# A hybrid attention and gating trunk on one core: forget gates, log-sum stores, output tiles' steps and the last row re-timed

## The chip, the core and the metric

The kernel runs on one core of a Trainium2 chip. The core has a matrix engine (PE, whose weight loads are listed as PEld), a vector engine (DVE), an activation engine (ACT), a general engine (POOL) and a sequencer (SP) that only issues transfers (DMAs). Each engine takes its instructions strictly in the order in which they stand in its queue, and waits where an operand or a buffer is not ready. The metric is the time of one execution in microseconds (us).

## The reference

One layer: an RMS norm and one input projection, then two token mixers side by side, one output projection of both with a residual, a SwiGLU feed-forward network with a residual, and a last RMS norm. There are 2048 tokens, 1024 features, 8 attention heads of 64, 8 gating groups of 64 and a hidden width of 2816. Everything is float32.

```python
xn = rms_norm(x, mix_norm_g[l])
q, k, v, f_logit, z = jnp.split(xn @ w_in[l], ...)
log_f = jax.nn.log_sigmoid(f_logit + b_f[l])
attn = forgetting_attention(q, k, v, log_f)      # softmax(q.k/8 + c[t] - c[s], s <= t) @ v, c = cumsum(log_f)
sgu = spatial_gating(gelu(z), sgu_ln_g[l], sgu_ln_b[l], w_s[l], b_s[l])
merged = concat([rms_norm(attn, out_norm_g[l, :512]), rms_norm(sgu, out_norm_g[l, 512:])])
x = x + merged @ w_out[l]
gate, up = jnp.split(rms_norm(x, ffn_norm_g[l]) @ w_gate_up[l], 2, axis=-1)
x = x + (silu(gate) * up) @ w_down[l]
return rms_norm(x, final_norm_g)
```

## The kernel before

A float32 operand is split into a high part (`hi_of`, a cast) and a low part (`lo_of`, the difference, line 131). A product takes three matmuls: high by high, high by low, low by high. The ACT mostly makes the high parts, the DVE the low ones. Python loops write the whole program out; a planner then sets the order of the instructions on each engine from its own model of their durations. `behind(i)` keeps what is written inside it behind instruction `i` on the same engine. Many helpers are Python generators: whoever calls `next` on one lets it write its instructions up to its next `yield`. So the number of `yield`s sets how many steps of the surrounding loop lie between two parts of a helper.

**Stage 1, the projection** (0 to about 315 us) takes four chunks `c` of 512 tokens. A chunk first makes its 8 rows of forget logits (lines 540 to 554) and stores them to `FD[c]` from ACT's queue. Then follow four tiles of q, four of k and, from the second chunk on, four of v, each 24 matmuls. After each tile `between` (line 430) moves two helpers by one step: `gates_`, which is `forget_rows(c)`, and `xg`, which prepares the next chunk's x (`Chunk.steps`, line 293). `forget_rows` loads the rows back as a tile `F` (line 315, issued by POOL) and computes the logarithm of the sigmoid on ACT and DVE (lines 320 to 328), later a cumulative sum on PE. In the meantime PE also takes, between the tiles' matmuls, the maxima of the chunk before (`one_max`, line 357): a matmul into one of two buffers `mx_ps`, and a DVE reduction (lines 362 and 365) that frees it.

**Stage 2** (to about 960 us) is 320 steps `n` (line 1242). A step is one key block of one head and query chunk: scores (`qk`, lines 735 and 736), an exponential and its two parts (738 to 742), a mask by POOL on the diagonal (748), and the products with v of the step before (`pv_of`, lines 768 to 773). Beside them run the gating branch (`gates`, with `z_proj`, `v_side` and `u_side`), and towards the end the output projection. When a head's query chunk is done, `fin` (line 777) copies the lower half of the sum (`lv`, whose first row is the log-sum's denominator), stores that row to `SD` from ACT's queue, and stores the numerator `nd` to `AT` from SP's. When all 8 heads of a query chunk `j` are done, it loads `SD[j]`, inverts it and stores it to `RD[j]`. `u_side` stores the transposed gating rows to `ST` from ACT's queue (line 1002).

From step `OPEN` = 260 on, two generators `out_prep(t, ...)`, for output tiles t = 0 and 1, move by one step each time (line 1295). Each loads `ST`, `AT` and, twice, `RD` (lines 1084 to 1089), multiplies (1092), squares on ACT (1094), adds on POOL (1097, 1098), sums over the partitions by a PE matmul (1111), takes the inverse root, and spreads it by a PE transpose (1116). For t = 0 and 1 the argument `space` is not None. `out_tiles` (line 1178) runs the output projection in groups of tiles; each of its group's 16 half steps moves the `out_prep` of the next tiles (t = 2 and 3 beside the first group) by one step.

**Stage 3, the feed-forward network** (to the end) uses 7 products in place of 8 for a 2 x 2 block product, n = 0 to 6 (line 1692). `Rows.evac(n)` adds a product into the rows `x`. The last group has a single item, for the rows t = 14 and 15. A finished row block goes to `Down.done`: the sum of its squares (ACT), an inverse root (DVE and POOL), a multiplication by it and by the norm's weights `finb` (DVE), and a store. t = 15 has its last addition at n = 5, t = 14 at n = 6; t = 14 is already treated in halves.

Of the kernel before, what the change touches and what calls it, by code (L numbers as in the profile page):

```python
# [8 lines left out]
F32 = mybir.dt.float32  # L9
F32R = mybir.dt.float32r  # L10
AF = mybir.ActivationFunctionType
ALU = mybir.AluOpType
# [4 lines left out]
P = 128  # L17
S = 2048
D = 1024
# [6 lines left out]
CH = 512  # L26
# [38 lines left out]
LEND = 276  # L65
LEAD = 14
ZF = 3
OPEN = 260
BURST = 6
ORATE = 2  # L70
FT = 9
# [4 lines left out]
NB = S // P  # L76
EPS = 1e-6
# [8 lines left out]
def trunk(ctx: ExitStack, tc: tile.TileContext, x, x_t, mix_g, w_in, b_f, ln_g, ln_b, w_st, b_st, on_g, w_out,  # L86
          ffn_g, w_gu, w_down, fin_g, c_mat, c_row, out):
    nc = tc.nc
# [4 lines left out]
    def T(pool, shape, dt, tag, **kw):  # L93
        n_t[0] += 1
        for tags, other in apart.get(id(pool), ()):
            if tag in tags:
                pool = other
        return pool.tile(shape, dt, tag=tag, name=f"{tag}_{n_t[0]}", **kw)
# [11 lines left out]
    def behind(*ins):  # L110

        s = ExitStack()
        for i in ins:
            s.enter_context(tc.issue_after(i.ins))
        return s
# [6 lines left out]
    ld = nc.sync.dma_start  # L122
# [36 lines left out]
    ST = [T(dram, [P, 4, P], F32, f"ST{t}") for t in range(NB)]  # L159
    AT = [T(dram, [P, 4, CH], F32, f"AT{c}") for c in range(NCH)]  # L160
    GD = [T(dram, [P, 4, CH], F32, f"GD{q}") for q in range(NCH)]
    SD = [T(dram, [H, CH], F32, f"SD{c}") for c in range(NCH)]
# [150 lines left out]
    def forget_rows(j):  # L313

        nc.gpsimd.dma_start(F[32 * j : 32 * j + 32, :], FD[j].rearrange("h (b t) -> b h t", t=P))
        for _ in range(1 if j else 2):
            yield
        sm = T(p1, [P, 8, P], F32, "v")
        ax, ex, u1, ln, er, ru, lf = (sm[:, i, :] for i in range(7))
        nc.scalar.activation(ax, F, AF.Abs)  # L320
        nc.scalar.activation(ex, ax, AF.Exp, scale=-1.0)
        nc.vector.tensor_scalar_add(u1, ex, 1.0)
        nc.scalar.activation(ln, u1, AF.Ln)
        nc.vector.scalar_tensor_tensor(er, u1, -1.0, ex, ALU.add, ALU.subtract)
        nc.vector.reciprocal(ru, u1)
        nc.vector.tensor_tensor(er, er, ru, ALU.mult)
        nc.vector.tensor_tensor(ln, ln, er, ALU.subtract)
        nc.vector.scalar_tensor_tensor(lf, F, 0.0, ln, ALU.min, ALU.subtract)
        for _ in range((3, 2, 1, 1)[j]):
            yield  # L330
        pl = T(ps1, [P, 4, P], F32, "tp")
        nc.tensor.transpose(pl[:, 0, :], lf, ident)
        sm2 = T(p1, [P, 4, P], F32, "fT", bufs=1)
        lfT, loc, nck = sm2[:, 0, :], sm2[:, 1, :], sm2[:, 2, :]
        nc.vector.tensor_copy(lfT, pl[:, 0, :])
        yield
        pl = T(ps1, [P, 4, P], F32, "tp")
        nc.tensor.matmul(pl[:, 1, :], lfT, tri, start=True, stop=True)
        nc.vector.tensor_copy(loc, pl[:, 1, :])
        yield  # L340
        pl = T(ps1, [P, 4, P], F32, "tp")
        nc.tensor.matmul(pl[:, 2, 0:1], cm[:, 1 + j, :], loc[:, P - 1 : P], start=True, stop=True)
        car = T(p1, [P, 1], F32, "car")
        nc.vector.tensor_copy(car, pl[:, 2, 0:1])
        nc.vector.tensor_scalar(nck, loc, car, -1.0, ALU.add, ALU.mult)
        augs = T(p1, [P, 2, P], F32R, "qh")
        nc.vector.tensor_copy(augs[:, 0, :], nck)
        lo_of(nc.vector, augs[:, 1, :], nck, augs[:, 0, :])
        n = 8 * (4 * j + 4)
        ldr(AUG[0:n, 2 * j : 2 * j + 2, :], augs[0:n])  # L350
# [185 lines left out]
    for c in range(NCH):  # L536
# [4 lines left out]
        n = 0  # L541
# [24 lines left out]
        for which, w in ((0, wq), (1, wk)):  # L566
            for pr in range(4):
                pm = T(ps1m, [P, CH], F32, "mm", bufs=4)
                n = 0
# [44 lines left out]
        for tt in range(4 if c else 0):  # L614
# [4 lines left out]
            a, b, _ = v_close(pm, xc, tt)  # L619
# [157 lines left out]
    def fin(h, j):  # L777
        pr, o = h // 2, (h % 2) * DH
        pv, _ = live.pop((h, j))
        nd, lv = T(p2, [DH, CH], F32, "nd", bufs=1), T(p2, [DH, CH], F32, "lv", bufs=1)  # L780
        nc.scalar.copy(lv, pv[DH:P])
        nc.scalar.dma_start(SD[j][h : h + 1], lv[0:1])
        nc.vector.scalar_tensor_tensor(nd, lv, m0[0:DH], pv[0:DH], ALU.mult, ALU.add)
        ld(AT[j][o : o + DH, pr, :], nd)
        heads[j] += 1
        if heads[j] == H:
            yield
            sr = T(p2, [P, H * CH // P], F32, "sr")
            ld(sr, SD[j].rearrange("h (a t) -> (h a) t", t=H * CH // P))
            yield  # L790
            yield
            yield
            nc.vector.reciprocal(sr, sr)
            ld(RD[j].rearrange("h (a t) -> (h a) t", t=H * CH // P), sr)
        yield
# [181 lines left out]
    def u_side(q, zr):  # L977

        yield
        yield  # L980
        ss = T(p2, [P, 4], F32, "ss2", bufs=1)
        m = mixes.pop(q)
        for cc in range(4):
            with behind(*newest):
                nc.vector.tensor_tensor(zr[:, cc, :], zr[:, cc, :], m[:, cc, :], ALU.mult)
                jk = T(p2, [P, CH], F32, "jk", bufs=1)
                nc.scalar.activation(jk, zr[:, cc, :], AF.Square, accum_out=ss[:, cc : cc + 1])
            yield
        rs = rsqrt(p2, ss, 1.0 / 512, "rs", n=4)
        yield  # L990
        last = q == NCH - 1
        if last:
            z4 = T(p2z, [P, 4, 4, P], F32, "zvh", bufs=1)
        for cc in range(4):
            nc.vector.tensor_scalar_mul(zr[:, cc, :], zr[:, cc, :], rs[:, cc : cc + 1])
            tp = T(ps2, [P, 4, P], F32, "mx_ps", bufs=NMX) if last else T(psz, [P, 4, P], F32, "z", bufs=NZ)
            for k in range(4):
                nc.tensor.transpose(tp[:, k, :], zr[:, cc, k * P : (k + 1) * P], ident)
            yield
            sT = z4[:, cc] if last else T(p2z, [P, 4, P], F32, ("wsth", "wstl")[cc % 2], bufs=1)  # L1000
            nc.scalar.copy(sT, tp)
            nc.scalar.dma_start(ST[4 * q + cc], sT)


    units = [(h, j) for h in range(H) for j in range(NCH)]
# [69 lines left out]
    first, o = [], [{} for _ in range(NB)]  # L1075

    def out_prep(t, o, space=None):
        c, sl = t // 4, slice((t % 4) * P, (t % 4 + 1) * P)
        r = raw4()
        if space is None:  # L1080
            rd = sq = T(pev, [P, 4, P], F32, "rd", bufs=3)
        else:
            rd, sq = space
        ld(r[:, 4:8, :], ST[t])
        ld(r[:, 0:4, :], AT[c][:, :, sl])

        for hh in range(2):
            ld(rd[hh * DH : (hh + 1) * DH],
               RD[c].rearrange("(pr o hh) t -> hh o pr t", hh=2, o=1)[hh, :, :, sl].broadcast_to([DH, 4, P]))
        for _ in range(4):  # L1090
            yield
        nc.vector.tensor_tensor(r[:, 0:4, :], r[:, 0:4, :], rd, ALU.mult)
        yield
# [11 lines left out]
            else:  # L1105
                ld(o["x"], x[t * P : (t + 1) * P, :])

        for _ in range(3 if space is None else 5):
            yield
        ps = E["tp"]()  # L1110
        nc.tensor.matmul(ps[:, 0, 0:1], sq[:, 0, :], ones_c, start=True, stop=True)
# [426 lines left out]
    class Down(Rows):  # L1538
# [18 lines left out]
        def evac(self, n):  # L1557
            super().evac(n)
            if (self.kb, self.tp, n) == (2, NB // 2 - 1, 3):

                xt = self.x[0][:, 0:CH]
                self.a = T(pev, [P, 1], F32, "a5")
                self.squares(xt, self.a)
                nc.vector.tensor_scalar(self.a, self.a, 1.0 / D, EPS, ALU.mult, ALU.add)
                nc.vector.tensor_tensor(xt, xt, finb[:, 0:CH], ALU.mult)

        def squares(self, xt, ss):
            jk = T(pev, [P, D], mybir.dt.bfloat16, "jk", bufs=1)
# [2 lines left out]
        def done(self, t, xt, at):  # L1571
            if self.kb < 2:
                ld(XA[t], xt)
                return
            ss = T(pev, [P, 1], F32, "ss4")
            o = out[t * P : (t + 1) * P, :]
            if t == NB - 2:
                right = xt[:, CH:]
                self.squares(right, ss)
                nc.vector.scalar_tensor_tensor(ss, ss, 1.0 / D, self.a, ALU.mult, ALU.add)  # L1580
                r = T(pev, [P, 1], F32, "r4r")
                nc.gpsimd.tensor_tensor(r, ss, mhalf[:, 0:1], ALU.pow)
                nc.vector.scalar_tensor_tensor(right, right, r, finb[:, CH:], ALU.mult, ALU.mult)
                ld(o[:, CH:], right)
                nc.scalar.activation(xt[:, 0:CH], xt[:, 0:CH], AF.Copy, scale=r)
                ld(o[:, 0:CH], xt[:, 0:CH])
                return
            while now[0] == at and at < len(grp) - 1:
                yield
            with behind(*copies if at < len(grp) - 1 else ()):  # L1590
                self.squares(xt, ss)
            yield
            r = rsqrt(pev, ss, 1.0 / D, "r4")
            if at == len(grp) - 1:
                yield
            nc.vector.scalar_tensor_tensor(xt, xt, r, finb, ALU.mult, ALU.mult)
            ld(o, xt)
            yield
# [93 lines left out]
    for q in range(len(slots)):  # L1692
# [35 lines left out]
            now[0] = p  # L1728
        tail = p == len(grp) - 1
        with behind(*[its[0].last] if tail and n else ()):  # L1730
            for _ in range((2, 2, 2, 2, 0, 1, 1)[n] if tail else len(its)):
                while posts and next(posts[0], 0) == 0:
                    posts.pop(0)
            if tail and n == 6:
                next(posts.pop(), None)
        if last:
            nextR[n] = next(fill)
        if sums and p:
# [50 lines left out]
```

## Time and profile before

| what | value |
|---|---|
| median of 3 runs | 2362.72 us (2359.24 to 2364.0) |
| the profiled execution's own time | 2363.86 us |
| its span, from first to last instruction | 2362.0 us |
| DVE busy | 1673.4 us (71%) |
| ACT busy | 1058.8 us (45%) |
| POOL busy | 609.8 us (26%) |
| bytes moved by DMA | 423.88 MB, mean 179 GB/s |
| mean granted PE clock | 0.998 of full |

The profile is of one execution. A row of the timeline gives the start and the duration in us, engine, line, operation, written and read tiles, shapes, and in brackets how long the engine was idle before and what ended that. "SPq" and "ACTq" are issues of transfers by those queues. A row of the waits gives the waiting instruction, what ended its waits, their sum in us, their number and the longest. A row of the windows gives the busy time of each engine in a stretch, with the number of instructions in brackets. A matmul is listed with about 0.39 us, but one starts about every 0.225 us.

### The profile page before, as it was taken

Reading aid. Unit: us, or ns where it says so; the run is one execution under the profiler, and the core shown is the slowest. Engines: PE = TensorE matmul, PEld = TensorE weight load, DVE = VectorE, ACT = ScalarE, POOL = GpSimd, SP = SyncE. Lnnn points to the kernel's source line nnn. Section 1 sums busy time; section 2 is a strip of 40 time slices with the busy share of each in tenths; the row PEclk is TensorE's granted clock in tenths of the full one; section 3 lists DMA queues with packets and bytes.
Section 4 is the critical chain, followed back from the end, with each engine's and each line's share of the span. In section 5 each row is a group of like instructions: output and inputs, shape, how many; then the busy total and the mean of one; then the engine's idle time right before and its main releaser. Section 6 shows DMA issues by size and latency. Waiting matters only on the chain.

```text
span 2362.0 us, 31692 instructions
## 1 busy us (share of the span) xinstructions
PE 2332.7 (99%) x10582; PEld 1893.4 (80%) x10582; DVE 1673.4 (71%) x2781; ACT 1058.8 (45%) x1771; POOL 609.8 (26%) x704
## 2 busy tenths in 40 slices
PE   9999999999999999999999999999999999999998
PEld 7787777777777777888888888888888888888886
DVE  6658668888888666566666666866666586685788
ACT  5322138777778766444323232532333252332433
POOL 1100012122211222221323223232323234353431
PEclk9999999999999999999999999999999999999999
DMA  8745667656677775674344544725454355574554
GB/s 271 282 153 200 203 198 210 186 152 170 178 201 241 222 227 171 212 222 153 108 142 148 164 143 125 230 82 148 120 152 134 98 187 192 189 257 169 190 195 149
DMA packets 375803, 423.88 MB, mean 179 GB/s; under 512 B 23941, under 2 KB 277573, under 8 KB 371673
## 3 DMA queue, kind: packets, MB, share of 16 engines
q1 hardware_dynamic: 359656, 378.62, 52.3%
q0 software_dynamic: 7616, 27.33, 3.3%
q10 hardware_dynamic: 8368, 15.91, 1.8%
q8 instruction: 85, 1.39, 0.2%
q14 instruction: 78, 0.63, 0.1%
HBM read 280.87 MB, written 140.91 MB: 179 GB/s over the span
## 4 chain that ended last, share of the span: by engine, by line
PE 86%; DVE 5%; DMA 4%; ACT 3%; issue 2%; POOL 1%; SPq 0%; ACTq 0%; POOLq 0%; DVEq 0%
PE pp L1718 51%; PE z L927 5%; PE mm L575 5%; PE pp L1176 4%; PE mm L457 3%; PE mx_ps L360 2%; PE tp L768 2%; PE tp L773 2%; PE mx_ps L735 2%; PE mx_ps L736 2%; PE oz L1176 2%; PE tp L770 1%; DVE wl L131 1%; DVE Pl L131 1%; PE z L968 0%
## 5 line engine op out<-in xcount | busy, mean ns | idle before, releaser
L128 ACT CAST wh<-raw 128x512 fp32r<-128x512 f32 (+2 forms) x492 | 303.4, 621 | 746.0 <-PE pp L1718 610.9
L131 DVE TENSOR_TENSOR wl<-raw,wh 128x512 fp32r<-128x512 f32 (+2 forms) x496 | 369.8, 754 | 27.6 <-ACT wh L128 27.0
L1718 PE MATMUL pp<-wl,wh 128*128 128x512 f32 x1056 | 325.5, 389 | 1.3 <-ACT u L1472 1.0
L1718 PE MATMUL pp<-wh,wh 128*128 128x512 f32 x1056 | 325.3, 389 | 0.0
L1415 POOL TENSOR_TENSOR raw<-raw 128x512 f32<-128x512 f32 (+1 forms) x124 | 173.0, 1397 | 565.4 <-DMA raw<-in_w_gu_dram 337.9
L131 DVE TENSOR_TENSOR Pl<-Pt,Ph 128x512 fp32r<-128x512 f32 (+1 forms) x320 | 195.2, 615 | 79.2 <-ACT Ph L128 75.0
L1718 PEld LDWEIGHTS pp<-wl,wh 128*128 128x128 f32 x1056 | 198.0, 188 | 43.6 <-ACT u L1472 1.4
L1718 PEld LDWEIGHTS pp<-wh,wh 128*128 128x128 f32 x1056 | 198.2, 188 | 41.2
L738 ACT ACTIVATE Pt<-mx_ps 128x512 f32<-128x512 f32 (+1 forms) x320 | 169.1, 532 | 122.0 <-PE mx_ps L736 117.7
L1718 PE MATMUL pp<-wl,wl 128*128 128x512 f32 x528 | 205.4, 389 | 0.0
L1718 PE MATMUL pp<-wh,wl 128*128 128x512 f32 x528 | 205.4, 389 | 0.0
L1415 DVE TENSOR_TENSOR raw<-raw,raw 128x512 f32<-128x512 f32 (+1 forms) x112 | 136.1, 1217 | 89.8 <-POOL raw L1415 86.5
L927 PE MATMUL z<-wh,xz 128*128 128x512 f32 x496 | 188.3, 396 | 0.0
L128 ACT CAST Ph<-Pt 128x512 fp32r<-128x512 f32 (+1 forms) x320 | 175.7, 556 | 19.6 <-PE tp L770 3.7
L362 DVE TENSOR_REDUCE mx<-mx_ps 128x1 f32<-128x512 f32 x192 | 130.0, 682 | 20.2 <-PE mx_ps L360 19.4
L748 POOL TENSOR_SCALAR_AFFINE_SELECT Ph<-Ph 128x128 fp32r<-128x128 f32 x128 | 50.2, 393 | 300.4 <-DVE Pl L131 215.5
L768 PE MATMUL tp<-Ph,V 128*128 128x512 f32 (+1 forms) x320 | 118.6, 371 | 4.6 <-POOL Ph L748 3.6
L773 PE MATMUL tp<-Pl,V 128*128 128x512 f32 (+1 forms) x320 | 118.4, 370 | 3.6 <-DVE Pl L131 2.5
L360 PE MATMUL mx_ps<-D,A 66*128 66x512 f32 (+2 forms) x320 | 118.6, 373 | 2.8 <-DVE mx L365 2.5
L735 PE MATMUL mx_ps<-A,D 74*128 74x512 f32 (+1 forms) x320 | 118.3, 370 | 0.5 <-ACT Pt L738 0.5
L736 PE MATMUL mx_ps<-B,C 128*128 128x512 f32 (+1 forms) x320 | 117.2, 367 | 0.0
L1718 PEld LDWEIGHTS pp<-wl,wl 128*128 128x128 f32 x528 | 99.1, 188 | 20.6
(352 smaller groups left out, 5282.4 us busy)
## 6 DMA issues: line engine op xcount, KB each, us to landing
raw<-in_w_gu_dram SPq DMA_DIRECT2D x88, 512.0 KB
xz<-XS SPq DMA_DIRECT2D x31, 1024.0 KB
HD<-hT SPq DMA_DIRECT2D x44, 512.0 KB
SM<-xa SPq DMA_DIRECT2D x30, 512.0 KB
D<-KH SPq DMA_DIRECT2D x112, 128.0 KB
XA<-xa SPq DMA_DIRECT2D x27, 512.0 KB
sg<-SM SPq DMA_DIRECT2D x12, 1024.0 KB
raw<-HD SPq DMA_DIRECT2D x24, 512.0 KB
```

What stands on the lines that cost most here:

```text
L128: return nc.scalar.copy(o, i) if eng is nc.scalar else eng.tensor_copy(o, i)
L131: return eng.tensor_tensor(o, i, f(h), ALU.subtract)
L360: last_mx.append(nc.tensor.matmul(pm[:, 0:n], lhs, Dt[0 : lhs.shape[0], 0:n], start=True, stop=True))
L735: nc.tensor.matmul(st[:, off:], Dt[:, b * P : (b + 1) * P], A[:, off:], start=True, stop=False)
L736: nc.tensor.matmul(st[:, off:], C[:, b * P : (b + 1) * P], B[:, off:], start=False, stop=True)
L738: nc.scalar.activation(Pt[:, off:], st[:, off:], AF.Exp)
L768: nc.tensor.matmul(pv[:, off:], V[:, 0:P], Ph[:, off:], start=kb == 0, stop=False)
L773: nc.tensor.matmul(pv[:, off:], V[:, 0:P], Pl[:, off:], start=False, stop=kb == 4 * j + 3)
L927: nc.tensor.matmul(pz, xz[a][:, k, :], w[b][:, k, :], start=n == 0, stop=n == 3 * KT - 1)
L1176: nc.tensor.matmul(ps, a, b, start=k == K_OUT[0] and e == 0, stop=k == K_OUT[-1] and e == 2)
L1415: return (nc.vector if e == "v" else nc.gpsimd).tensor_tensor(o, a, b, op)
L1718: nc.tensor.matmul(pm, a[:, k, :], b[:, k, :], start=on is None and k == 0 and e == 0, stop=k == it.kh - 1 and e == 2, skip_group_check=n ...
```

## The change

Four things are changed. In `forget_rows` the work on `F` comes two tiles after its load in every chunk, where it came one tile after it in all but the first. The store of the log-sum row in `fin` is issued by SP, after the multiplication that makes `nd`; the gating stores of the last quarter are issued by SP as well. `OPEN` becomes 256; with `space` given, `ST` and `AT` are loaded in steps of their own, three more steps lie ahead of the loads of `RD` and one more behind them; tiles 2 and 3 get two more steps before the multiplication and two more before the partition sum. In the last group, t = 15 is treated in halves like t = 14: its right half is squared and multiplied by `finb` at n = 4, and the closing work of both row blocks is put in a new order.

```diff
-OPEN = 260
+OPEN = 256
...
         nc.gpsimd.dma_start(F[32 * j : 32 * j + 32, :], FD[j].rearrange("h (b t) -> b h t", t=P))
-        for _ in range(1 if j else 2):
-            yield
+        yield
+        yield
...
         nc.scalar.copy(lv, pv[DH:P])
-        nc.scalar.dma_start(SD[j][h : h + 1], lv[0:1])
         nc.vector.scalar_tensor_tensor(nd, lv, m0[0:DH], pv[0:DH], ALU.mult, ALU.add)
+        ld(SD[j][h : h + 1], lv[0:1])
         ld(AT[j][o : o + DH, pr, :], nd)
...
-            nc.scalar.dma_start(ST[4 * q + cc], sT)
+            (nc.sync if last else nc.scalar).dma_start(ST[4 * q + cc], sT)
...
         ld(r[:, 4:8, :], ST[t])
+        if space is not None:
+            yield
         ld(r[:, 0:4, :], AT[c][:, :, sl])
-
+        for _ in range(0 if space is None else 3):
+            yield
         for hh in range(2):
             ld(rd[hh * DH : (hh + 1) * DH],
...
-        for _ in range(4):
+        for _ in range(6 if t in (2, 3) else 4 if space is None else 5):
             yield
         nc.vector.tensor_tensor(r[:, 0:4, :], r[:, 0:4, :], rd, ALU.mult)
...
-        for _ in range(3 if space is None else 5):
+        for _ in range(3 if t > 3 else 5):
             yield
...
+            if (self.kb, self.tp, n) == (2, NB // 2 - 1, 4):
+
+                xt = self.x[1][:, CH:]
+                self.b = T(pev, [P, 1], F32, "b5")
+                self.squares(xt, self.b)
+                nc.vector.tensor_scalar(self.b, self.b, 1.0 / D, EPS, ALU.mult, ALU.add)
+                nc.vector.tensor_tensor(xt, xt, finb[:, CH:], ALU.mult)
...
-            if t == NB - 2:
-                right = xt[:, CH:]
-                self.squares(right, ss)
-                nc.vector.scalar_tensor_tensor(ss, ss, 1.0 / D, self.a, ALU.mult, ALU.add)
+            if t >= NB - 2:
+                at, by, c = (slice(CH, D), slice(0, CH), self.a) if t == NB - 2 else (slice(0, CH), slice(CH, D), self.b)
+                self.squares(xt[:, at], ss)
+                self.last = nc.vector.scalar_tensor_tensor(ss, ss, 1.0 / D, c, ALU.mult, ALU.add)
                 r = T(pev, [P, 1], F32, "r4r")
                 nc.gpsimd.tensor_tensor(r, ss, mhalf[:, 0:1], ALU.pow)
-                nc.vector.scalar_tensor_tensor(right, right, r, finb[:, CH:], ALU.mult, ALU.mult)
-                ld(o[:, CH:], right)
-                nc.scalar.activation(xt[:, 0:CH], xt[:, 0:CH], AF.Copy, scale=r)
-                ld(o[:, 0:CH], xt[:, 0:CH])
+                yield
+                nc.vector.scalar_tensor_tensor(xt[:, at], xt[:, at], r, finb[:, at], ALU.mult, ALU.mult)
+                ld(o[:, at], xt[:, at])
+                nc.scalar.activation(xt[:, by], xt[:, by], AF.Copy, scale=r)
+                ld(o[:, by], xt[:, by])
                 return
...
-            for _ in range((2, 2, 2, 2, 0, 1, 1)[n] if tail else len(its)):
+            for _ in range((2, 2, 2, 2, 0, 1, 0)[n] if tail else len(its)):
                 while posts and next(posts[0], 0) == 0:
                     posts.pop(0)
-            if tail and n == 6:
-                next(posts.pop(), None)
+        if tail and n == 6:
+            next(posts[1])
+            with behind(its[0].last):
+                next(posts.pop(0), None)
```

More of the change, by code (lines that the diff above doesn't have):

```diff
@@ L1576, in done @@
             o = out[t * P : (t + 1) * P, :]
-            if t == NB - 2:
-                right = xt[:, CH:]
-                self.squares(right, ss)
-                nc.vector.scalar_tensor_tensor(ss, ss, 1.0 / D, self.a, ALU.mult, ALU.add)
+            if t >= NB - 2:
+                at, by, c = (slice(CH, D), slice(0, CH), self.a) if t == NB - 2 else (slice(0, CH), slice(CH, D), self.b)
+                self.squares(xt[:, at], ss)
+                self.last = nc.vector.scalar_tensor_tensor(ss, ss, 1.0 / D, c, ALU.mult, ALU.add)
                 r = T(pev, [P, 1], F32, "r4r")
                 nc.gpsimd.tensor_tensor(r, ss, mhalf[:, 0:1], ALU.pow)
-                nc.vector.scalar_tensor_tensor(right, right, r, finb[:, CH:], ALU.mult, ALU.mult)
-                ld(o[:, CH:], right)
-                nc.scalar.activation(xt[:, 0:CH], xt[:, 0:CH], AF.Copy, scale=r)
-                ld(o[:, 0:CH], xt[:, 0:CH])
+                yield
[3 more added lines that the diff above has]
+                ld(o[:, by], xt[:, by])
                 return
-            while now[0] == at and at < len(grp) - 1:
+            while now[0] == at:
                 yield
-            with behind(*copies if at < len(grp) - 1 else ()):
+            with behind(*copies):
                 self.squares(xt, ss)
@@ L1593, in done @@
             r = rsqrt(pev, ss, 1.0 / D, "r4")
-            if at == len(grp) - 1:
-                yield
             nc.vector.scalar_tensor_tensor(xt, xt, r, finb, ALU.mult, ALU.mult)
```

## The prediction

> **What bounds the kernel now.** I read the busy shares first, then what PE waited for, and then the timeline around each of the longer waits.
>
> ```profile
> span 2362.0 us, 31692 instructions
> ...
> PE 2332.7 (99%) x10582; PEld 1893.4 (80%) x10582; DVE 1673.4 (71%) x2781; ACT 1058.8 (45%) x1771; POOL 609.8 (26%) x704
> PE tp L768 <- POOL Ph L748: 3.6, 8, 1.1
> PE mx_ps L1111 <- POOL rd L1098: 2.6, 2, 1.4
> PE tp L773 <- DVE Pl L131: 2.5, 2, 1.9
> PE mx_ps L360 <- DVE mx L365: 2.5, 1, 2.5
> ...
> PE mx_ps L1111 <- POOL zvl L1098: 0.8, 1, 0.8
> ```
>
> PE is busy for 2332.7 of 2362.0 us, so 29.3 us are all that can be won without fewer matmuls, and the change takes none away. The named waits are few. The change touches five: 2.5 (L360), 2.5 and 0.8 (L773 and L1111 of the first two output tiles), 2.6 (L1111 of tiles 2 and 3), and one of 1.1 in the first row, 9.5 us together. The rest of the idle time that matters is the end, after the last matmul.
>
> **Forget gates.** The wait at L360 belongs to the second chunk:
>
> ```profile
> 94.20 0.31 ACT L320 ACTIVATE v<-F 128x128 f32<-128x128 f32 x1 [4.09 <-DMA F<-FD]
> 94.53 1.28 ACT L321 ACT_TABLE_LOAD   x1
> 96.16 0.23 DVE L322 TENSOR_SCALAR v<-v 128x128 f32<-128x128 f32 x1 [4.67 <-ACT v L321]
> 98.05 0.47 PE L360 MATMUL mx_ps<-D,A 66*128 66x128 f32 x1 [2.49 <-DVE mx L365]
> ...
> 96.00:99.00 3.00, 0.00 (x0) 0.00 (x0) 2.25 (x6) 0.44 (x2) 0.00 (x0) 0.83 0.50 177
> 99.45:105.50 6.05, 6.05 (x26) 4.83 (x25) 5.21 (x18) 2.92 (x4) 1.06 (x2) 0.84 0.61 234
> ```
>
> ACT stands 4.09 us before the tile F has landed, DVE stands 4.67 us behind ACT, and the reductions that free `mx_ps` stand behind DVE's instruction: PE loses 2.49 us. One tile later F has long landed, so that wait goes. What is late next is DVE itself. The gates' DVE work is 2.25 us (first window, tile v alone), and it moves into the tile from 99.45 to 105.50 (second window), where DVE already works 5.21 of 6.05 us on the next chunk's halves: 7.46 in 6.05, an arrear of 1.4 us. In the third and fourth chunk it is the same:
>
> ```profile
> 179.87:187.00 7.13, 7.13 (x36) 5.92 (x35) 6.69 (x20) 2.92 (x4) 1.17 (x3) 1.00 0.70 249
> 267.00:274.00 7.00, 7.00 (x34) 5.64 (x33) 6.03 (x15) 0.66 (x2) 1.07 (x2) 1.00 0.77 270
> ```
>
> 6.69 + 2.25 in 7.13 is 1.8 us over, 6.03 + 2.25 in 7.00 is 1.3 us over. How much PE bears? In the quoted case DVE lost 4.67 us and PE 2.49, so some 2.2 us of arrears cost nothing. All three lie below that, the middle one closely. Bounds: -2.5 if all is covered, +2.0 (1.4 + 1.8 + 1.3 - 2.5) if nothing is. I take -2.2, near the covered end, as each arrear is under 2.2. The matmuls that follow (L332 to L342) and the store of AUG come one tile later, which the remaining tiles of the chunk hide.
>
> **Stores moved to SP.** One wait of PE on the mask (L748) began with a store on ACT's queue:
>
> ```profile
> 707.87 0.24 ACTq L782 DMA_DIRECT2D SD<-lv  x1
> 708.21 0.41 ACT L128 CAST Ph<-Pt 128x256 fp32r<-128x256 f32 x1 [2.07 <-DMA D<-AUG]
> 709.62 0.38 PE L768 MATMUL tp<-Ph,V 128*128 128x256 f32 x1 [1.12 <-POOL Ph L748]
> ...
> L782 ACTq DMA_DIRECT2D SD<-lv x32: 221/222/244, 339.3 to 959.4; - x32
> L784 SPq DMA_DIRECT2D AT<-nd x32: 460/466/1937, 343.6 to 961.7; - x32
> ```
>
> The issue of SD waited until an unrelated transfer (D<-AUG) had landed, with the cast of Ph behind it, then DVE, POOL and PE: 1.12 us. With the store on SP that hold falls on the load queue. Bounds: -1.1, or 0 if another hold takes its place; I take -1.0. On SP 32 issues of 0.22 to 0.47 us are added, at most 15 us of 620, and each stands ahead of the AT store, which waits for later data anyway. The inversion now follows SD on one queue. The four gating stores (12 stay on ACT) were not held: 0.
>
> [...] Here the 2.07 us hold on ACT shows a cost beyond the 0.24 us of issue.
>
> **First output tiles.**
>
> ```profile
> 829.66 1.29 SPq L1088 DMA_DIRECT2D zvl<-RD  x2
> 831.90 0.69 DVE L1092 TENSOR_TENSOR raw<-raw,zvl 128x512 f32<-128x512 f32 x1 [3.78 <-DMA zvl<-RD]
> 833.25 0.50 PE L773 MATMUL tp<-Pl,V 128*128 128x512 f32 x1 [1.88 <-DVE Pl L131]
> 839.19 0.38 PE L1111 MATMUL mx_ps<-ones_c,zvl 128*128 128x1 f32 x2 [0.76 <-POOL zvl L1098]
> ...
> 872.62 1.34 SPq L1088 DMA_DIRECT2D rd<-RD  x2
> 880.82 0.69 DVE L1092 TENSOR_TENSOR raw<-raw,rd 128x512 f32<-128x512 f32 x1 [1.08 <-DMA rd<-RD]
> 883.57 0.38 PE L1111 MATMUL mx_ps<-ones_c,rd 128*128 128x1 f32 x2 [1.14 <-POOL rd L1098]
> 888.09 0.38 PE L1111 MATMUL mx_ps<-ones_c,rd 128*128 128x1 f32 x2 [1.44 <-POOL rd L1098]
> ...
> 870.15 0.40 PE L735 MATMUL mx_ps<-A,D 74*128 74x512 f32 x1
> 884.58 0.40 PE L735 MATMUL mx_ps<-A,D 74*128 74x512 f32 x1
> ```
>
> For t = 0 and 1, all eight loads start in one step, the last two of RD at 829.66, and DVE stands 3.78 us for them with Pl behind it. After the change ST and AT start 4 and 3 steps earlier, RD in the old step (256 + 1 + 3 = 260) with nothing else, and the multiplication one step later (265 for 264). The waits are worth 2.5 + 0.8 = 3.3; bounds -3.3 and 0 (RD as late as now). I take -2.8: four of eight transfers leave the crowd, and a step is over 2 us (the last two rows are the first and the last of seven L735, one a step: 14.43 us for 6 steps, 2.4 each).
>
> For t = 2 and 3, L1111 moves back by 2 + 2 half steps. With two half steps in a step of 2.4 us it has 4.8 us more against waits of 1.14 and 1.44: both go, -2.6. What is late next: tile 2 has 16 half steps, its transpose now falls into the last of them and its splits right ahead of its first matmul. A split is a cast and a subtraction of 512 columns, by the rows of the end below some 0.63 us on ACT and 0.68 on DVE, behind the same pair for the current Ph and Pl: 0 to 2.0 us of new wait (three such, in part side by side). I take 0.6, as the planner can put the next scores ahead. Net -2.0.
>
> **The end.**
>
> ```profile
> 2352.00 0.39 PE L1718 MATMUL pp<-wl,wl 128*128 128x512 f32 x1
> 2352.54 0.68 DVE L1487 TENSOR_TENSOR sg<-sg,pp 128x512 f32<-128x512 f32 x1
> 2352.70 1.06 ACT L1569 ACTIVATE jk<-sg 128x1024 bf16<-128x1024 f32 x1 [6.39 <-issue]
> 2353.88 0.63 ACT L1569 ACTIVATE jk<-sg 128x512 bf16<-128x512 f32 x1
> 2354.18 0.55 POOL L176 TENSOR_TENSOR r4r<-r4a,mhalf 128x1 f32<-128x1 f32 x1 [6.12 <-DVE r4a L174]
> 2354.77 1.28 DVE L1596 SCALAR_TENSOR_TENSOR sg<-sg,r4r,sg 128x1024 f32<-128x1024 f32 x1 [0.73 <-POOL r4r L176]
> 2356.85 0.75 DVE L1583 SCALAR_TENSOR_TENSOR sg<-sg,r4r,sg 128x512 f32<-128x512 f32 x1 [0.73 <-POOL r4r L1582]
> 2357.63 0.33 SPq L1584 DMA_DIRECT2D out_dram<-sg  x1
> 2358.05 0.38 SPq L1586 DMA_DIRECT2D out_dram<-sg  x1
> ```
>
> From the last issue (2358.05) to the end (2362.0) are 3.95 us, which stay. Ahead of it, t = 14 stands behind t = 15 on ACT (1.06) and DVE (1.28). After the change both squares are of 512: ACT from 2352.70 to 2353.5 and on to 2354.2 (0.63 each, and the read of the sum). The new multiplication by `finb` adds 0.7 us to DVE behind L1487, to 2353.9. From a square's end to its factor are 1.01 us now (2353.76 to 2354.77), so the factors come at about 2354.7 and 2355.2. DVE multiplies 0.75 + 0.75 to 2356.2, ACT the other halves beside it, and SP issues four stores 0.42 us apart, the last at 2356.6: -1.4. Bounds: -1.8 (the `finb` product hidden) and -0.5.
>
> [...]
>
> **The sum.** -2.2 - 1.0 - 2.8 - 2.0 - 1.4 = -9.4 us. The planner deals the order anew wherever the change reaches, and about 9 us of the named waits are not among mine; I add 1.0 for new ones (estimate, bounds -2 and +4). That leaves -8.4: 2355.5 for the profiled execution (2363.86, span 2362.0 and 1.9 around it), and 2354.3 against the median 2362.72, 1.1 lower than that execution.
>
> **Rivals.**
> 1. *The loads stay late.* If the RD loads, early or not, queue behind other transfers, the output tiles' terms vanish (-2.8 and -2.0): -8.4 + 4.8 = -3.6, 2359.1. For it: RD took until 880.8 though tile 2's were issued some 8 us before. Against it: PE asks 4.8 us later for tiles 2 and 3 whatever the loads do. Chance 0.11.
> 2. *Halves at the end waste bandwidth.* Two stores of 256 KB for one of 512 KB; if each half costs its 0.42 us of issue again at the end, 0.8 of the 1.4 goes: 2355.1. Against it: the two halves of t = 14 are issued 0.42 us apart now, and the end still follows the second by only 3.95 us. Chance 0.04.
> 3. *DVE becomes the bound at the gates.* The arrears of 1.4, 1.8 and 1.3 are borne by PE in full: +2.0 for -2.2, 2358.5. The third chunk's 6.69 of 7.13 speaks for it, the 2.2 us of cover against. Chance 0.09.
> 4. *SP falls behind: slower.* Place: the loads of xz for the gating matmuls, which would stand behind SD on SP.
>
> ```profile
> xz<-XS SPq DMA_DIRECT2D x31, 1024.0 KB
> ```
>
> Now PE waits for none. SP's longest hold at an AT store is 1.94 us (L784). If the holds at SD run on so that each xz is 0.5 us late, PE loses 31 x 0.5 = 15.5: -8.4 + 15.5 = +7.1, 2369.8. It decides once SP's added delay exceeds the time for which an xz load lies ready. Against it: SD waits only for what AT waits for anyway. Chance 0.06.
>
> My own forecast has 0.70. **Chances**: 0.2% is 4.7 us, about what a measurement of this kernel can tell. Faster by more (below 2358.0): 0.70 + 0.04 + part of the others, 0.75; within it: most of rivals 1 and 3, 0.18; slower: rival 4 and a dear new order, 0.07. **Range**: 2350.5 (2362.72 less 9.5 of waits, 1.8 at the end and 1 of the others) to 2361.0 (rival 1 with costs of the new order).
>
> **What would show it.** L360's wait of 2.5 gone and no DVE-ended wait over 0.7 near 187 or 274; no ACT hold ended by a DMA at a store of SD; no wait of L1111 on POOL; tile 2's first matmuls waiting under 1 us; the last issue some 4.6 us after the start of the last matmul, where it is 6.05 now (2352.00 to 2358.05). Wrong I would be if waits of like size stood in new places of stage 2, or if SP's holds grew.

## The result, and the profile after

| | before | after |
|---|---|---|
| median of 6 runs each | 2362.97 us (2359.24 to 2364.23) | 2375.16 us (2370.97 to 2377.41) |
| ratio of the times | 1 | 1.0050, 95% interval 1.0037 to 1.0063 |
| profiled execution, its span | 2363.86, 2362.0 us | 2377.41, 2375.5 us |
| mean granted PE clock of that execution | 0.998 | 0.996 |

The change makes the kernel 12 us slower; 8.4 us faster was forecast. The page of after has the same matmuls, and PE stands idle for 37.0 us of its span, 7.7 more than before:

```profile
span 2375.5 us, 31692 instructions
...
PE 2338.5 (98%) x10582; PEld 1895.5 (80%) x10582; DVE 1671.6 (70%) x2783; ACT 1059.1 (45%) x1774; POOL 611.4 (26%) x704
```

Busy time grew as well, by 5.8 us. Some 3.4 us of that is the same work at a lower granted clock (last section); the rest was not followed. What PE waited for in after (L1114 is L1111 of before, L1119 is L1116):

```profile
PE tp L768 <- POOL Ph L748: 4.0, 6, 1.4
PE mx_ps L1114 <- POOL zvl L1101: 2.7, 2, 1.8
PE mx_ps L1114 <- POOL rd L1101: 2.7, 2, 2.1
PE z L927 <- DMA xz<-XS: 2.4, 1, 2.4
PE tp L773 <- POOL Pl L748: 2.0, 4, 1.4
...
PE tp L1119 <- POOL rar L176: 1.4, 1, 1.4
```

The waits of L1114 that were to go are still there, and there are new ones of xz and L1119. To see where the time was lost I followed the start of the same matmul in both traces. After minus before, it is -2.3 us when the projection ends, -0.4 at the scores near 745 us, +10.7 at those near 916 us, +13.6 at 1100 us. Most is lost between 745 and 916 us, at the first output tiles. There SP's own waits are telling (the waiting issue, what ended its waits, their sum, number and longest). After:

```profile
SPq L783 <- ACT lv L781: 38.0, 19, 6.2
SPq L784 <- DVE nd L782: 15.1, 13, 2.6
SPq L794 <- DVE sr L793: 13.9, 4, 7.2
SPq L1002 <- ACT zvh L1001: 10.6, 1, 10.6
```

Before:

```profile
SPq L784 <- DVE nd L783: 24.1, 15, 3.5
SPq L794 <- DVE sr L793: 8.6, 3, 4.4
```

L783 is the new issue of SD, L784 that of AT, L794 the store of RD, L1002 the gating store. The waits named here came to 32.7 us and come to 77.6. And this is SP's order in after, at the first output tiles:

```profile
797.99 0.56 SPq L125 DMA_DIRECT2D xz<-XS  x1
804.30 0.22 SPq L783 DMA_DIRECT2D SD<-lv  x1
806.87 0.46 SPq L784 DMA_DIRECT2D AT<-nd  x1
...
808.59 0.35 SPq L789 DMA_DIRECT2D sr<-SD  x1
...
817.89 0.35 SPq L794 DMA_DIRECT2D RD<-sr  x1
...
827.95 0.57 SPq L125 DMA_DIRECT2D xz<-XS  x1
828.57 2.90 SPq L904 DMA_DIRECT2D zvh<-GD  x1
831.51 2.59 SPq L1091 DMA_DIRECT2D zvl<-RD  x4
...
835.33 0.76 PE L927 MATMUL z<-wh,xz 128*128 128x512 f32 x1 [2.39 <-DMA xz<-XS]
845.45 0.38 PE L1114 MATMUL mx_ps<-ones_c,zvl 128*128 128x1 f32 x2 [1.79 <-POOL zvl L1101]
848.25 0.38 PE L1114 MATMUL mx_ps<-ones_c,zvl 128*128 128x1 f32 x2 [0.93 <-POOL zvl L1101]
```

From 798.6 to 804.3 SP stands at SD, and the rest of the chain (sr, RD, the loads of RD) follows late: RD is loaded at 831.51, where before the first of these four loads was issued at 821.0. A natural reading is that SP's holds are the whole cause. The experiments show that it is not so.

### The profile page after: what moved, and what is told of

Same layout as the page of the kernel before. It is cut to its first block, busy times and chain, and to the rows that moved or that the text cites. A ratio compares the mean times of both kernels' runs of the same rounds, so it can differ in the third digit from the quotient of the medians.

```text
span 2375.5 us, 31692 instructions
## 1 busy us (share of the span) xinstructions
PE 2338.5 (98%) x10582; PEld 1895.5 (80%) x10582; DVE 1671.6 (70%) x2783; ACT 1059.1 (45%) x1774; POOL 611.4 (26%) x704
## 4 chain that ended last, share of the span: by engine, by line
PE 70%; DVE 5%; ACT 3%; issue 2%; POOL 2%; DMA 1%; POOLq 0%; SPq 0%; DVEq 0%; ACTq 0%
PE pp L1727 51%; PE z L927 4%; PE pp L1179 3%; PE oz L1179 2%; PE tp L773 2%; PE tp L768 2%; PE mx_ps L735 2%; PE mx_ps L736 2%; PE tp L770 1%; DVE Pl L131 1%; PE mx_ps L360 1%; DVE wl L131 1%; ACT Pt L738 1%; PE z L968 1%; ACT Ph L128 0%
## 5 line engine op out<-in xcount | busy, mean ns | idle before, releaser
L768 PE MATMUL tp<-Ph,V 128*128 128x512 f32 (+1 forms) x320 | 119.2, 373 | 4.5 <-POOL Ph L748 4.0
L360 PE MATMUL mx_ps<-D,A 66*128 66x512 f32 (+2 forms) x320 | 119.0, 375 | 3.3 <-DVE mx L365 1.5
```

Of the source, the lines that this page charges most:

```text
L360: last_mx.append(nc.tensor.matmul(pm[:, 0:n], lhs, Dt[0 : lhs.shape[0], 0:n], start=True, stop=True))
L768: nc.tensor.matmul(pv[:, off:], V[:, 0:P], Ph[:, off:], start=kb == 0, stop=False)
```

## The experiments

Each was timed against the kernel before on the same chip, in five rounds. The chips differ from group to group, so two runs are compared below by their ratios.

| run | what it is | median, us | ratio to before, 95% interval |
|---|---|---|---|
| no_stores | changed kernel, stores on ACT | 2358.1 | 0.9984 (0.9975 to 0.9993) |
| stores | before, stores SD and ST on SP | 2373.3 | 1.0048 (1.0035 to 1.0062) |
| steps | before, output tiles' steps | 2361.4 | 0.9998 (0.9989 to 1.0006) |
| gates_end | before, gates and end | 2361.5 | 0.9991 (0.9982 to 1.0000) |
| sd_only | before, SD on SP | 2368.6 | 1.0023 (1.0014 to 1.0032) |
| st_only | before, last ST on SP | 2363.4 | 1.0001 (0.9992 to 1.0010) |
| sd_after_at | as sd_only, SD behind AT | 2370.4 | 1.0027 (1.0017 to 1.0038) |
| sd_pool | before, SD on POOL | 2370.7 | 1.0028 (1.0016 to 1.0040) |
| stores_old_order | stores, order of before | 2368.8 | 1.0018 (1.0010 to 1.0027) |
| old_stores_new_order | before, order of stores | 2378.7 | 1.0054 (1.0039 to 1.0069) |
| after_old_order | after, order of no_stores | 2365.7 | 1.0003 (0.9993 to 1.0012) |
| sd_old_order | sd_only, order of before | 2366.0 | 1.0009 (1.0000 to 1.0018) |
| stores_early | stores, lv, nd, sr put back | 2383.7 | 1.0079 (1.0065 to 1.0093) |
| no_st_old_order | after, ST on ACT, order of no_stores | 2357.9 | 0.9978 (0.9968 to 0.9988) |
| after_st_late | after_old_order, ST later on SP | 2363.3 | 1.0002 (0.9993 to 1.0011) |
| stores_at_old | stores, SD and AT put back on SP | 2377.2 | 1.0059 (1.0047 to 1.0071) |
| before_at_new | before, AT put forward on SP | 2364.3 | 1.0003 (0.9994 to 1.0011) |

### Which part of the change

Four runs take the change apart. The first takes back only these two places of it, the second makes only these:

```diff
         nc.scalar.copy(lv, pv[DH:P])
+        nc.scalar.dma_start(SD[j][h : h + 1], lv[0:1])
         nc.vector.scalar_tensor_tensor(nd, lv, m0[0:DH], pv[0:DH], ALU.mult, ALU.add)
-        ld(SD[j][h : h + 1], lv[0:1])
...
-            (nc.sync if last else nc.scalar).dma_start(ST[4 * q + cc], sT)
+            nc.scalar.dma_start(ST[4 * q + cc], sT)
```

> The changed kernel with SD and the last ST stores back on ACT's queue (gates, steps and end kept). Theory A (the stores on SP hold its queue, so the loads of the first output tiles come late): the loss between 745 and 915 us goes, 11 us of 12.2; time 2355 to 2361 us, RD loads of tiles 0 and 1 issued before 825 us, no half-clock stretch more than before (2 of 3.4 us). Theory B (the moved steps of the output tiles are the cause): 2372 to 2376. Theory C (any edit makes the planner deal a new order, with new waits): anywhere, with the loss in other places.

> The kernel before with only SD and the last ST stores moved to SP. Theory A: 8 to 12 us slower, 2371 to 2375, with SP holds behind lv of 5 us and more. Theory B: within 2 us of before, 2361 to 2365. Theory C: 0 to 5 us slower.

The other two make, on the kernel before, only the edits of `OPEN` and `out_prep`, and only those of `forget_rows` and of the last group, as the change has them:

> The kernel before with only the steps of the output tiles moved (OPEN 256 and all the yields). Theory A: the waits of tiles 0 to 3 go as predicted, 2 to 5 us faster, 2358 to 2361. Theory B: 8 to 12 us slower, 2371 to 2375. Theory C: between.

> The kernel before with only the forget gates' extra tile and the new end. Theories A and B: -2.2 at the end of the projection and -0.7 at the end, 2.9 us faster, 2360.0. Theory C: the gain of 2.2 us is spent again in the first half of stage 2 (as in the changed kernel, where it stood at 0.4 by 745 us), 2362.

The stores cost it: alone they make the kernel slower by as much as the whole change, and without them the rest is faster than before (3.8 us by the ratio, 1.7 to 5.9). The moved steps cost nothing, so Theory B falls, and they bring nothing that can be told. Theory A named the right part; that SP's holds are the reason was not yet shown.

### Which store, and which queue

> The kernel before with only the log-sum row's store (SD) issued by SP. Theory A1 (SP stands at SD until lv is there, and the loads behind it come late): most of the 10.5 us that both stores cost together, 2369 to 2373. Theory A2 (SD no longer on ACT lets the planner place lv itself later on ACT, so the chain lv, SD, sr, RD is late at its start): the same, 2369 to 2373. Theory B (the gating store, held 11 us on SP, does it): 2361 to 2365.

> The kernel before with only the last four gating stores (ST) issued by SP. Theories A1 and A2: 0 to 3 us slower, 2362 to 2366. Theory B: 8 to 11 us slower, 2370 to 2374.

They make one each of the two edits of the run stores. The next two put SD elsewhere; the first diff is against sd_only, the second against the kernel before:

```diff
-        ld(SD[j][h : h + 1], lv[0:1])
         ld(AT[j][o : o + DH, pr, :], nd)
+        ld(SD[j][h : h + 1], lv[0:1])
```

```diff
-        nc.scalar.dma_start(SD[j][h : h + 1], lv[0:1])
+        nc.gpsimd.dma_start(SD[j][h : h + 1], lv[0:1])
```

> As sd_only, but SD is issued behind the store AT of the same head on SP, so that the row lv has always been copied when SP comes to SD. Theory A1: SP's holds at SD go and those at AT stay about as before (24 us in all), 2361 to 2365. Theory A2: lv stays late on ACT and the loss stays, 2369 to 2373. Theory B: 2361 to 2365.

> The kernel before with SD issued by POOL, so neither ACT nor SP has it. Theory A1: SP's queue is as before, 2360 to 2364, 0 to 2 us better if ACT's hold of 2.07 us is gone without a price. Theory A2: lv is late here too, 2368 to 2373. Theory B: 2361 to 2364.

SD costs 5 to 7 us wherever it goes, even on POOL, where SP has nothing new to wait for. Theory A1 falls as the whole cause. ST alone costs nothing, though SP stood 9.8 us at it in that run; together with SD it adds some 6 us to what SD costs alone (1.0048 less 1.0023), which no run here explains. The three times of SD are near what Theory A2 expected, a later `lv` on ACT; it is tried again below, as Theory L. What the three SD runs share is that SD has left ACT's queue. Their orders, set beside that of before, differ on PE, DVE and ACT too: in the trace of stores 390 of PE's 10582 places hold another instruction (by operation and tile) than in that of before, 173 of DVE's 2781 and 124 of ACT's 1745. So the planner's order itself had to be tried.

### Order and queue apart

In the next runs the order of each of the five queues is pinned. Every instruction gets an edge to the one that stood ahead of it in the recorded order of another kernel, so the planner has no choice left (`want` holds the recorded places, `made` the instructions of a queue as they were written out):

```diff
+        for e, steps in want.items():
+            at, seq = 0, []
+            for k, step in enumerate(steps):
+                at += step + 1
+                seq.append(made[e][at - 1])
+            for a, b in zip(seq, seq[1:]):
+                tc.add_manual_dep(b, a.name, _mybir.DependencyInfo(_mybir.DependencyClass.NoSync, _mybir.DependencyReason.DATA), reason="order")
```

Only the moved stores are set in anew: SD right ahead of its AT on SP, or right behind its copy on ACT.

> SD and the last four ST issued by SP, as in the run stores, but every other instruction of all five queues pinned to the order of the kernel before; SD stands right ahead of AT of its head. Theory Q (what the stores cost is SP standing at them): 2370 to 2375, as in the run stores. Theory R (the move lets the planner deal another order on PE, DVE and ACT, and that order is the worse one): 2361 to 2365, equal to before.

> The stores on ACT's queue as before, each right behind the copy that it stores, but every other instruction pinned to the order that the planner dealt in the run stores. Theory Q: SP is free of the holds, 2361 to 2365. Theory R: the order is kept and so is its loss, 2370 to 2375.

> The whole changed kernel, stores on SP, but all other instructions pinned to the order of the run no_stores. Theory Q: 2370 to 2376, about the changed kernel. Theory R: 2356 to 2360, about the run no_stores (2358.1).

Both kernels of the first pair are slower, but not alike. The new order, with every store on ACT as before, costs the whole loss and more (12.8 us); the move with the old order costs 4.3 us. So Theory R carries most and Theory Q a part. The third run says the same of the changed kernel: of the 16 us between after (1.0050) and no_stores (0.9984) the order of no_stores wins back 11 (1.0003). Pinning by itself costs nothing that shows: before_at_new, whose order is that of before but for a few stores, has 1.0003. The profile of old_stores_new_order shows the waits of the run after at the same instructions, with no SD on SP:

```profile
847.23 0.38 PE L1111 MATMUL mx_ps<-ones_c,zvl 128*128 128x1 f32 x2 [2.64 <-POOL zvl L1098]
...
886.76 0.80 PE L768 MATMUL tp<-Ph,V 128*128 128x512 f32 x1 [1.41 <-POOL Ph L748]
903.44 0.53 PE L1111 MATMUL mx_ps<-ones_c,rd 128*128 128x1 f32 x2 [2.08 <-POOL rd L1098]
```

And SP still waits long there, now at AT and at RD:

```profile
SPq L784 <- DVE nd L783: 33.3, 15, 3.8
SPq L794 <- DVE sr L793: 20.4, 4, 8.8
```

So long holds on SP are in good part a sign of the order: SP's issues and the instructions that they wait for were dealt to places that do not fit each other.

The 12.8 us are not all the loss of the run stores, though. From the scores near 745 us to the last matmul the trace of old_stores_new_order falls 10.7 us behind before, that of stores 10.7 as well, that of stores_old_order 4.6. But old_stores_new_order is 6.5 us late already near 745 us, where stores is 0.9 late; 1.9 of them come near 98 us, with a longer wait of L360 (the longest of that line is 3.1 us, 2.5 in before), and the mean granted clock of that execution is 0.994, where before has 0.998. These are single executions, and they scatter: that of before_at_new falls 4.9 us behind on the same stretch, with a median like that of before. So the sizes are rough, and the shares of order and holds do not add up to the whole.

### What of the queue, what of the order

> Only SD on SP, right ahead of AT; everything else in the order of the kernel before. Theory S (SP's holds at SD cost time): 2367 to 2370. Theory G (only the gating stores' hold of 12.5 us costs, as it stands ahead of the loads of tile 2): 2361.5 to 2364.5, equal to before or up to 1 us below it (ACT's hold of 2.07 us at SD gone).

> The run stores with its whole order pinned, but the copies lv of three heads, the multiplications nd of eight and two inversions sr put back behind the instruction that they follow in the kernel before. Theory L (the late start of the chain lv, SD, sr, RD is what the new order costs): 2364 to 2368, 5 us or more below the run stores (2373.3). Theory M (many small changes of the order on PE and DVE cost it, here and there): 2370 to 2375.

> Gates, steps, end and SD on SP, ST left on ACT, in the order of the run no_stores (2358.1). Theory G: 2356 to 2359. Theory S: 2361 to 2364.

SD on SP with the old order costs 2.1 us (0 to 4.3); in the order of no_stores it costs nothing (0.9978 beside 0.9984). Theory G holds in the second case, and the first does not decide. The gating stores do cost something in the order of no_stores: with them on SP after_old_order has 1.0003, without them no_st_old_order 0.9978. In the order of before the same step (1.0018 beside 1.0009) can't be told from none. In after_old_order SP stands at them for 13.2 us, and the first load of tile 2 (`raw<-ST`) leaves at 873.04:

```profile
SPq L1002 <- ACT zvh L1001: 13.2, 1, 13.2
...
866.10 0.81 SPq L1002 DMA_DIRECT2D ST<-zvh  x2
...
873.04 0.45 SPq L1084 DMA_DIRECT2D raw<-ST  x1
```

With the stores on ACT, in no_st_old_order, it leaves at 868.89. Theory L was not borne out: with lv, nd and the inversions put back the kernel became 7 us slower still than the run stores (1.0079 beside 1.0048). The test is not clean, though, and leaves Theory L open. SP's second load of sr was left late (851.94, before 835.59), so the inversion put forward on DVE (L793) had to wait for it with all work of DVE behind it:

```profile
851.94 0.35 SPq L789 DMA_DIRECT2D sr<-SD  x1
...
853.72 0.35 DVE L793 RECIPROCAL sr<-sr 128x32 f32<-128x32 f32 x1 [3.42 <-DMA sr<-SD]
```

The last three runs move a few issues on SP and nothing else.

> As after_old_order (2365.7), but the last four gating stores stand 9 to 15 places later on SP, behind the first loads of output tile 2. Theory H (SP's hold of 13.2 us at them, with the loads of tile 2 and the key blocks behind it, is their cost): the hold shrinks below 3 us and the time falls to 2357 to 2360, as in no_st_old_order (2357.9). Theory N (something else about the stores): 2363 to 2367.

> As the run stores (2373.3) with its order pinned, but the stores SD and AT that stand earlier on SP than in the kernel before are put back to their old places there. Theory H2 (their early place on SP, with SP held at them for 34.7 + 18.3 us, is what the new order costs): 2363 to 2367. Theory M (the order on PE, DVE and ACT costs it): 2370 to 2375, with the holds at SD and AT smaller all the same.

> The kernel before with its order pinned, but AT on SP at the earlier places that it has in the run stores; SD stays on ACT. Theory H2: 5 us or more slower, 2368 to 2373. Theory M: within 2 us of before, 2361 to 2365.

In after_st_late the hold is gone from the list of waits, and the time is the same as with it (1.0002 and 1.0003). The four issues take 2.69 us there, and the loads of RD that follow leave at 874.63, where in no_st_old_order they leave at 871.68:

```profile
867.66 2.69 SPq L1002 DMA_DIRECT2D ST<-zvh  x4
...
874.63 1.27 SPq L1091 DMA_DIRECT2D rd<-RD  x2
```

So Theory H is not borne out: four issues ahead of late loads remained, with or without the long hold. Theory H2 fell twice. With SD and AT back in their places SP's hold at SD shrank from 34.7 to 13.4 us and the kernel stayed as slow; AT put forward cost nothing. What is left is the order of everything else. That is the order on PE, DVE and ACT, Theory M, but also that of SP's loads, which no run put back: between the pinned lists of stores_old_order and stores_at_old 74 of SP's 1326 issues still have to change places, some 68 of them neither SD nor AT, and more than half of these loads of key blocks. Which of the moved instructions costs the time stays open; no run exchanges the order of one engine alone.

The fastest kernel of the study is no_st_old_order: the changed kernel with ST on ACT in the order of no_stores, 0.9978 of before, 5.2 us (2.8 to 7.6, by the interval). Against no_stores the difference is not resolved.

## Why the prediction was wrong

**Stores moved to SP** is the step that failed, and with it the term for the new order. The text said of SD "each stands ahead of the AT store, which waits for later data anyway", took -1.0 with bounds -1.1 and 0, and gave all parts together +1.0 for the planner's new order with bounds -2 and +4. Measured alone the move costs 11.3 us (8.3 to 14.7); with the old order it costs 4.3, so most of it comes with the new order, which was priced with a lump sum of at most 4 for all parts.

The gain of 1.0 us was not there to be won either. The hold of 2.07 us on ACT at the store of SD, with the wait of 1.12 us of L768 behind it, stands in the one trace of before and in no other. In before_at_new the store is on ACT too, and ACT and PE have the order of before; there the issue follows its copy, and the cast has no wait:

```profile
704.24 0.58 ACT L781 COPY lv<-tp 64x512 f32<-64x512 f32 x1
...
704.85 0.24 ACTq L782 DMA_DIRECT2D SD<-lv  x1
...
705.32 0.41 ACT L128 CAST Ph<-Pt 128x256 fp32r<-128x256 f32 x1
```

In steps, st_only, gates_end and no_stores, all with SD on ACT, it is the same. These five and sd_old_order, with SD on SP, alike gain 1.4 us on the trace of before between the scores at 707.87 and those at 710.09 us. So the term priced an accident of one execution; why it stood there is open.

"The four gating stores were not held: 0" was wrong too: on SP they were held 10.6 us, a wait that did not exist where they stood. By themselves they cost nothing (st_only), in the pinned order of no_stores some 6 us (1.0003 less 0.9978).

**Rival 4**, SP falls behind, had the right sign and a chance of 0.06. Its place shows once (xz late, 2.39 us at 835.33), not 31 times. Against it the text set that SP's longest hold at an AT store was 1.94 us. That is the duration of the longest issue; the list of waits of before has one of 3.5 us there, and 24.1 us in all. With the old order kept, the issues and holds added to SP are worth some 4 us of the 11 (stores_old_order), and no wait of PE for xz stands in that trace. That the order is dealt anew, which carries most of the rest, stood in the sum and in a chance, but was no rival with a place and a price, and should have been one.

**Forget gates**: -2.2 was forecast, and at the end of the projection the trace of gates_end is 2.4 us ahead, that of after 2.3. The sum is right, its parts are not. DVE's arrears were to cost PE next to nothing (0.3 us); in the trace of after they cost 0.83, 0.43 and 1.03 us:

```profile
102.63 0.33 PE L360 MATMUL mx_ps<-D,A 66*128 66x128 f32 x1 [0.83 <-DVE mx L365]
...
183.27 0.51 PE L360 MATMUL mx_ps<-D,A 66*128 66x512 f32 x1 [0.43 <-DVE mx L365]
196.10 0.51 PE L360 MATMUL mx_ps<-D,A 66*128 66x512 f32 x1 [1.03 <-DVE mx L362]
```

That is 2.3 us against the 2.5 that went. What made the term come out was a stretch at half clock behind the old wait, worth 1.7 us, that went with it in these executions. That is luck.

**First output tiles**: -2.8 and -2.0 were forecast; the run steps as a whole gives -0.5 us (-2.6 to +1.4). Most of the waits did not go, they moved on to the next instruction of the same chain: PE's waits of over 0.5 us at these tiles come to 5.9 us in before and to 3.8 in steps. In the trace of steps:

```profile
820.89 5.92 SPq L1091 DMA_DIRECT2D zvl<-RD  x4
...
831.23 0.69 DVE L1095 TENSOR_TENSOR raw<-raw,zvl 128x512 f32<-128x512 f32 x1 [1.48 <-DMA zvl<-RD]
...
836.02 0.50 PE L773 MATMUL tp<-Pl,V 128*128 128x512 f32 x1 [1.66 <-DVE Pl L131]
...
889.51 0.32 PE L1119 MATMUL mx_ps<-ident,rar 128*128 128x128 f32 x1 [1.23 <-POOL rar L176]
```

The four loads of RD leave from 820.89 to 826.81, earlier than before (821.03 to 830.95), yet the multiplication still waits for them, 1.48 for 3.78 us. Then the two tiles' DVE work comes close together and PE waits 1.66 us for Pl. For tiles 2 and 3 L1111 (L1114 here) no longer waits, as forecast, but the transpose behind it waits 1.23 us for the root. The step "both go" looked at one instruction of the chain and not at its next. This one execution is 3.7 us ahead of before from 745 us on, 1.7 of them a stretch at half clock that it does not have (0.50 from 889.90 to 893.30 us in before, 1.00 from 889 to 893 in steps); the eleven executions of steps together don't show that gain.

**The end**: -1.4 was forecast. The last issue comes 5.65 us after the start of the last matmul (6.05 before, 4.6 forecast), and the span ends 9.34 us after it (10.0 before): a gain of 0.7, and half the size.

```profile
2366.20 0.39 PE L1727 MATMUL pp<-wl,wl 128*128 128x512 f32 x1
2366.43 0.68 DVE L1575 TENSOR_TENSOR sg<-sg,sg 128x512 f32<-128x512 f32 x1
2367.03 0.68 DVE L1418 TENSOR_TENSOR sg<-sg,u 128x512 f32<-128x512 f32 x1
2367.64 0.68 DVE L1490 TENSOR_TENSOR sg<-sg,pp 128x512 f32<-128x512 f32 x1
2367.81 0.63 ACT L1579 ACTIVATE jk<-sg 128x512 bf16<-128x512 f32 x1 [1.48 <-DVE sg L1418]
2368.57 0.63 ACT L1579 ACTIVATE jk<-sg 128x512 bf16<-128x512 f32 x1
...
2371.85 0.40 SPq L1597 DMA_DIRECT2D out_dram<-sg  x1
```

The new product with `finb` (L1575) stands on DVE ahead of two additions that the squares need. The squares were to start 0.70 us after the last matmul; the first starts 1.61 us after it. The stores in halves cost nothing that shows (the end follows the last issue by 3.69 us, 3.95 in before), so rival 2 fell; rivals 1 and 3 each hold in part (RD was still late, DVE's arrears were paid).

By these runs the parts come to +8.7 us (stores 11.3, steps -0.5, gates and end -2.1), where 12 were measured for the whole; the gap of 3 is no larger than the intervals of the parts.

## What to carry to other kernels

Where a planner orders the instructions, moving even a small transfer to another queue is a change of the order on every engine: compare the orders first, and pin the old one to measure the move by itself. A long hold of a queue may be the sign of a bad order rather than the cause of the loss; move the held issue alone before believing it. When a wait is taken away, price the next consumer of the same chain, and the clock behind the wait. And before a wait is priced, look for it in a second trace of the same order: one that stands in a single execution may be an accident of it.

## What the runs showed of the hardware

By some of PE's waits of one microsecond and more lies a stretch of 3.41 us at a granted clock of 0.50; half of 3.41, another 1.7 us, is my estimate of what it takes from the matmuls. The windows (busy times with numbers of instructions, then the granted clock, DMA share and GB/s) of after:

```profile
834.90:838.30 3.40, 2.97 (x7) 2.42 (x8) 0.00 (x0) 0.46 (x1) 0.00 (x0) 0.50 1.11 270
...
899.70:903.10 3.40, 3.40 (x10) 2.51 (x11) 2.11 (x5) 0.67 (x2) 0.00 (x0) 0.51 0.57 133
```

They lie at waits of 2.39 us (at 835.33) and 2.07 us (at 899.59). Between the first and the last microseconds of the span the trace of after has four such stretches, at 834.90, 848.55, 882.69 and 899.75 us, beside seven waits of 1.0 us or more; that of before has two, at 97.98 and 889.88 us, beside five. So by the estimate 3.4 of the 13.5 us between the spans are clock. Like waits come with a stretch and without one. The wait of L360 near 98 us was 2.49 us in before and 2.47 us in steps; the first window is of before, with 9 matmuls, the second of steps, with 15:

```profile
98.00:101.40 3.40, 3.35 (x9) 2.77 (x10) 3.08 (x12) 1.23 (x3) 0.00 (x0) 0.50 0.00 0
```

```profile
97.90:101.40 3.50, 3.30 (x15) 2.67 (x16) 3.17 (x14) 1.18 (x3) 0.00 (x0) 1.00 0.00 1
```

In after the waits of 1.03, 1.35 and 1.44 us (at 196.10, 423.42 and 1034.97) have no stretch, and one begins 0.3 us behind a wait of 0.93 us (that at 848.25). The four stretches of after start 4, 10 and 5 times 3.41 us apart. The scatter between executions goes with the clock: of the runs of before beside these experiments, those with a mean clock of 0.995 have a mean span of 2364.5 us, those with 0.998 one of 2360.0. What decides whether a wait is joined by a stretch was not shown.
